# One encoder layer on one core: the mixer's projections as split fp32r pieces, with its other work cut into steps

## The chip, the cores and the metric

The kernel runs on one core of a Trainium2 chip. The core's engines work side by side, each through a queue of its own in order: TensorE (PE, with its weight loads as PEld), VectorE (DVE), ScalarE (ACT), GpSimd (POOL), and SyncE (SP), which here issues DMAs. The metric is the device time of one execution in microseconds (us): 2279.44 us before the change (median of 3 runs, 2277.18 to 2281.16).

## What is computed

One layer of a hybrid encoder on 256 tokens of width 2048, in float32:

```
h = rmsnorm(x);  p = h @ w_in                      # 5248 columns
z, q, k, v = split(p)
y_rwkv = rwkv7_bidir(z, ...)                       # 16 heads x 64, forward + backward delta-rule scans
y_attn = axial_gqa(q, k, v, ...)                   # 16 query heads, 4 kv heads, dim 64, softmax over 256
x = x + concat(y_rwkv, y_attn) @ w_out
x = x + peer_ffn(rmsnorm(x))                       # 8 heads, top 16 of 128 x 128 experts each
out = rmsnorm(x)

# in rwkv7_bidir, for each token and head (state is 64 x 64):
sa = state @ -kk;  state = state * w + outer(sa, ka) + outer(v, k);  y = state @ r
```

Everything up to `@ w_out` is called the mixer here, what follows PEER. In `peer_ffn` the kernel multiplies with all expert rows and weighs them by a gate, so PEER is two large dense products (`u` and `v`).

## The kernel before

**Layout.** Activations lie with features on the 128 partitions and the 256 tokens along the free axis. A weight block of 128 output columns is contracted over 2048 inputs in 16 steps k.

**The mixer before.** Its products are plain float32. `proj` (line 274) makes one block of 128 columns: four loads of 256 KB (`rw`), and 16 matmuls of a 128x128 weight with the 128x256 tokens `xy` into a PSUM tile `pj`. The trace has two records for each float32 matmul, so a block is 32 records. There are 40 such blocks of `w_in`; `proj_v` (335) does the work of two more for the value columns; `wout_block` (711) and `late` (787) do the 16 blocks of `w_out`, each contraction in four quarters, added one by one on DVE to the residual tiles `h`. The last quarter is `late`.

Between the projections stands the mixer's other work, small matmuls in float32 and DVE and ACT instructions:
- `shifted` (403): scale by 1/rms (`z`), then the centred token shift (`zk`, `zr`, `zv`), on DVE and ACT.
- `prep` (456), for each of 4 units of 4 heads, 2 directions and 2 halves (16 passes): decays (`sg`, `cs`, `Pt`, `iP`), in-context rates (`av`), scaled keys `AK` and queries `pk`, their chunk products, masks (`pk<-pr`, `Ld`, `L`) and transposes; results go to DRAM (`D`, `V`).
- `inverse` (545): a 32x32 triangular inverse, 30 dependent pairs of DVE instructions on tiles `h`; `merge` (562) makes 64x64 inverses from it with 128 small matmuls. Both run twice.
- `chain` (589): the scan over 4 chunks of 64 tokens, for two units (8 heads in both directions) at a time; each chunk loads `PK` and `VV` from DRAM and needs the state `N` of the chunk ahead. It runs twice (C0, C1). `epilogue` (645) is group norm, bonus and gate.
- `attend` (395): per group of 4 heads, `scores` and `values`: scores in PSUM, maximum on DVE, exponentials `pe` on ACT, transposes on PE, copy `pt` on ACT, product with the values.

**What sets the order in the mixer.** The string `ORDER` (line 39) gives the order in which these parts are written, and that order is the priority of a list scheduler in the compiler, which places each engine's instructions by its own estimate of their ends. Nothing in the mixer is ordered by hand.

**PEER.** From line 736 on the queues follow the order as written. The weights come in pieces of 512 KB (`raw`). A piece is split before use into two fp32r parts: ACT writes the rounded part `wH` (`wH<-raw`), POOL or DVE the rest `wL` (`wL<-raw,wH`). `mm3` (209) then makes a product from three fp32r matmuls, weight and token operand each in a high and a low part (high times high, high times low, low times high). `wide` (821) does it with a 512-column and a 256-column matmul. `go` (764) keeps `AHEAD` = 3 pieces split and `RAWB` = 4 more loaded ahead of the one in use.

Of the kernel before, what the change touches and what calls it, by code (L numbers as in the profile page):

```python
# [132 lines left out]

def body(tc, a, out, dbg={}):
    nc = tc.nc
    V, S, G, T = nc.vector, nc.scalar, nc.gpsimd, nc.tensor
# [97 lines left out]

# [7 lines left out]
    pss = bank("pt")[:, 0:2]  # L242
    pro = tc.tile_pool(name="pro", bufs=1, side="right")
    wp = pro.__enter__()
    xrs = [wp.tile([128, 4, 256], F, name="xr", bufs=4) for c in range(4)]
    for c in range(4):
        nc.sync.dma_start(xrs[c], a["xT"][:, 4 * c:4 * c + 4, :])
    nc.sync.dma_start(cst, a["cst"])
    for c in range(4):
        xr = xrs[c]  # L250
        tt(V if c < 2 else G, xA[:, 4 * c:4 * c + 4], xr,
           Pm("n1", 4 * c, 4)[:, :, None].to_broadcast([128, 4, 256]), OP.mult)
    for c in range(4):
# [3 lines left out]
        V.tensor_reduce(sm, sq.rearrange("p k t -> p t k"), axis=AX.X, op=OP.add)
        for b in range(2):
            mm(pss[:, b:b + 1], sm[:, b * 128:(b + 1) * 128], ones[:, 0:1], c + b == 0, c == 3)
    rstd = const.tile([128, 2, 1], F)  # L260
    rsqrt(wp, rstd[:, :, 0], pss, 2, 1.0 / 2048, 1e-6)
    psb = bank("pt")[:, :256]
    spread(psb, rstd.to_broadcast([128, 2, 128]))
    act(rstdb, psb)
    pro.__exit__(None, None, None)

    dr = pool("dr", 1, DRAM)
    ldp = pool("ldp", 1, side="right")
    rwc = pool("rwc", 1, side="right")
    at = pool("at", side="right")  # L270
    wk = pool("wk", 1)
    two = lambda p: p.rearrange("p (a b) -> p a b", a=2)

    def proj(n):
        p = pp.tile([128, 256], F, name="pj")
        for c in range(4):
# [5 lines left out]
    def headscale(pl, sq, scale, add, guard=None, tag="s2", bt="pr"):  # L282

        p = bank(bt)[:, :8].rearrange("p (b i h) -> p b i h", b=2, i=2)
        for b in range(2):
            for i in range(2):
                mm(p[:, b, i], sq[:, i, b * 128:(b + 1) * 128], bones[:, 0:128:64], b + i == 0, True)
        s1 = pl.tile([128, 8], F, name="s1")
        rsqrt(pl, s1, p.rearrange("p b i h -> p (b i h)"), 8, scale, add, guard)
        s2 = pl.tile([128, 8, 64], F, name=tag, bufs=2 if tag == "w2" else 1)  # L290
        V.tensor_copy(s2, s1[:, :, None].to_broadcast([128, 8, 64]))
        s2 = s2.rearrange("p (b i h) n -> p b i (h n)", b=2, i=2)
        p = bank(bt).rearrange("p (a b) -> p a b", a=2)
        for i in range(2):
            spread(p[:, i], s2[:, :, i])
        return p


    rope = at.tile([128, 768], F, name="rope")
    RP = {"rot": rope[:, 0:128], "swp": rope[:, 128:256], "cos": rope[:, 256:512], "sin": rope[:, 512:768]}  # L300
    c2 = lambda n: RP[n][:, None, :].to_broadcast([128, 2, 256])

    zA = at.tile([128, 5, 2, 256], F, name="zA")
    kW = at.tile([128, 2, 256], F, name="kW")
    vA = at.tile([128, 2, 256], F, name="vA")

    def proj_attn(n):
        for i in range(2):
            p = proj(30 + 2 * n + i)
            tt(V, zA[:, n, i], p, rstdb, OP.mult)  # L310

    def qk_block(n, w, bt):

        zs = zA[:, n]
        q = at.tile([128, 2, 256], F, name="aq")
        act(q, zs, AF.Square)
        V.tensor_scalar(zs, zs, w, None, op0=OP.mult)
        tt(V, zs, zs, headscale(at, q, 1.0 / 64, 1e-6, bt=bt, tag="aq"), OP.mult)
        p = bank(bt)
        mm(p, RP["rot"], zs)  # L320
        q = at.tile([128, 2, 256], F, name="aq")
        tt(V, q, two(p), c2("sin"), OP.mult)
        tt(V, zs, zs, c2("cos"), OP.mult)
        tt(V, zs, zs, q, OP.add)

    def keys(bt):
        nc.sync.dma_start(rope, a["rope"])
        qk_block(4, Pm("kn"), bt)
        p = bank(bt)
        mm(p, RP["swp"], zA[:, 4])  # L330
        act(kW, two(p))
        tap("kA", zA[:, 4])
        tap("vA", vA)

    def proj_v():
        pv2 = [pp.tile([128, 256], F, name="pj") for _ in range(2)]
        for c in range(8):
            W = wload(a["wv"][:, 2 * c:2 * c + 2, :].rearrange("p a (b n) -> p (a b) n", b=2))
            W = W.rearrange("p (a b) n -> p a (b n)", b=2)
            for b in range(2):  # L340
                for k in range(2):
# [6 lines left out]
    pes, sms, pys = {}, {}, {}

    def scores(e, bt):  # L350
        g, hq = divmod(e, 4)
        i, h = divmod(hq, 2)
        s = slice(64 * h, 64 * h + 64)
        kt = zA[s, 4, g // 2] if g % 2 == h else kW[s, g // 2]
        if hq == 0:
            sms[g] = at.tile([128, 2, 4], F, name="sm", bufs=2)
        p = two(bank(bt))
        for b in range(2):
            mm(p[:, b], zA[s, g, i, b * 128:(b + 1) * 128], kt)
        mx = at.tile([128, 2], F, name="mx", bufs=2)  # L360
        V.tensor_reduce(mx, p, axis=AX.X, op=OP.max)
        V.tensor_scalar(mx, mx, -0.125, None, op0=OP.mult)
        pes[e] = at.tile([128, 2, 256], F, name="pe", bufs=2)
        for b in range(2):
            act(pes[e][:, b], p[:, b], AF.Exp, scale=0.125, bias=mx[:, b:b + 1],
                accum_out=sms[g][:, b, hq:hq + 1])
# [53 lines left out]

# [828 lines left out]
```

## Time and profile before

| | us |
|---|---|
| median of the runs | 2279.44 |
| the profiled execution | 2277.42 |
| its span, first to last instruction | 2275.6 |
| PE busy in the span | 2214.7 |
| DVE busy | 1223.4 |
| ACT busy | 961.8 |
| POOL busy | 823.6 |
| first product of PEER (a matmul on `hh`) | at 664.5 |

The profile's page groups the instructions by line, engine and operation; most lines are those of helpers (158 for matmuls, 161 for ACT, 164 for DVE and POOL), so the tile names tell the groups apart. Busy times of PE are those of pipelined instructions that overlap, and say less than the distance from one start to the next.

### The profile page before, as it was taken

To read this page: it belongs to the slowest core of one execution; us is meant where nothing else is said; L and a number is where in the kernel's file an instruction comes from. 1 tells how busy PE (TensorE), PEld (TensorE's weight loads), DVE (VectorE), ACT (ScalarE), POOL (GpSimd) and SP (SyncE) were. 2 spreads that over 40 slices of the span, in tenths; PEclk is the share of its full clock that TensorE was granted. 3 is DMA by queue.
4 is the path that set the end of the run, shared out by engine and by line. 5 is a ranking of instruction groups with operands and counts; after the bars stand their busy time and mean duration, and the time that the engine had idled before them with its cause. 6 is when DMAs were issued, how large, how long until landed. Compare 5 with 4: busy or idle time off the path is not lost.

```text
span 2275.6 us, 33493 instructions
## 1 busy us (share of the span) xinstructions
PE 2214.7 (97%) x12790; PEld 1883.2 (83%) x12790; DVE 1223.4 (54%) x2556; ACT 961.8 (42%) x1479; POOL 823.6 (36%) x377
## 2 busy tenths in 40 slices
PE   7999799899999999999999999999999999999997
PEld 6888688787878889999888888888888888887886
DVE  3365875675367788887443352342533433456654
ACT  1121222323137755555544444444444444444443
POOL 0000000000027600000755555555555555556554
PEclk9999799699999999999999999999999999999999
DMA  5465364275455546666756666566566566676674
GB/s 196 148 188 174 127 196 146 82 240 174 138 183 170 174 160 221 213 209 215 240 189 205 203 194 209 190 203 212 187 211 205 185 211 205 194 229 212 207 209 133
DMA packets 188832, 431.50 MB, mean 190 GB/s; under 512 B 39680, under 2 KB 82304, under 8 KB 184448
## 3 DMA queue, kind: packets, MB, share of 16 engines
q1 hardware_dynamic: 177376, 409.96, 57.2%
q10 hardware_dynamic: 11296, 19.40, 2.5%
q8 instruction: 101, 1.65, 0.3%
q14 instruction: 59, 0.48, 0.1%
HBM read 391.55 MB, written 37.75 MB: 189 GB/s over the span
## 4 chain that ended last, share of the span: by engine, by line
PE 91%; DVE 5%; ACT 1%; DMA 1%; issue 1%; ACTq 0%; SPq 0%; DVEq 0%
PE pc L158 37%; PE pj L158 33%; PE pr L158 19%; PE pt L158 1%; DVE wL L164 1%; DVE oh L164 1%; ACT wH L161 0%; PE pr L532 0%; DMA VV<-V 0%; DVE pk L164 0%; DVE xy L164 0%; DVE hh L807 0%; DVE AK L164 0%; DVE h L164 0%; DVE rs L164 0%
## 5 line engine op out<-in xcount | busy, mean ns | idle before, releaser
L164 POOL TENSOR_TENSOR wL<-raw,wH 128x1024 fp32r<-128x1024 f32 x328 | 798.3, 2438 | 1018.5 <-ACT wH L161 1011.9
L161 ACT ACTIVATE wH<-raw 128x1024 fp32r<-128x1024 f32 x544 | 575.4, 1060 | 456.3 <-PE pc L158 282.8
L164 DVE TENSOR_TENSOR wL<-raw,wH 128x1024 fp32r<-128x1024 f32 x216 | 274.1, 1269 | 347.4 <-ACT wH L161 347.3
L158 PE MATMUL pr<-hh,wH 128*128 128x512 f32 x1152 | 409.3, 396 | 0.2 <-ACT wH L161 0.2
L158 PE MATMUL pj<-hh,wH 128*128 128x512 f32 x1152 | 408.0, 395 | 1.5 <-DVE hh L807 1.3
L158 PE MATMUL pc<-wH,aH 128*128 128x512 f32 x1024 | 406.7, 397 | 1.1 <-DVE acc L164 1.1
L158 PE MATMUL pc<-wH,aL 128*128 128x512 f32 x1024 | 404.8, 395 | 0.0
L158 PE MATMUL pc<-wL,aH 128*128 128x512 f32 x1024 | 402.0, 393 | 0.0
L158 PE MATMUL pj<-xy,rw 128*128 128x256 f32 x1664 | 382.6, 386 | 0.0
L158 PEld LDWEIGHTS pj<-xy,rw 128*128 128x128 f32 x1664 | 316.6, 193 | 49.6 <-issue 4.7
L158 PE MATMUL pr<-hh,wL 128*128 128x256 f32 x1152 | 323.1, 281 | 1.4 <-DVE wL L164 1.4
L158 PE MATMUL pj<-hh,wL 128*128 128x256 f32 x1152 | 322.1, 280 | 0.0
L158 PEld LDWEIGHTS pj<-hh,wH 128*128 128x128 f32 x1152 | 216.4, 188 | 48.4 <-DVE hh L807 2.0
L158 PEld LDWEIGHTS pr<-hh,wH 128*128 128x128 f32 x1152 | 217.2, 189 | 46.6 <-ACT wH L161 0.5
L158 PEld LDWEIGHTS pc<-wH,aL 128*128 128x128 f32 x1024 | 192.2, 188 | 48.3
L158 PEld LDWEIGHTS pc<-wL,aH 128*128 128x128 f32 x1024 | 192.3, 188 | 46.6
L158 PEld LDWEIGHTS pc<-wH,aH 128*128 128x128 f32 x1024 | 192.2, 188 | 46.1 <-DVE acc L164 1.5
L158 PEld LDWEIGHTS pr<-hh,wL 128*128 128x128 f32 x1152 | 217.2, 189 | 2.4 <-DVE wL L164 2.4
L158 PEld LDWEIGHTS pj<-hh,wL 128*128 128x128 f32 x1152 | 216.5, 188 | 0.4
L164 DVE TENSOR_TENSOR acc<-pc,acc 128x512 f32<-128x512 f32 x128 | 86.2, 688 | 131.6 <-PE pc L158 131.6
L504 POOL COPY vp<-zv 128x256 f32<-128x256 f32 x16 | 7.7, 482 | 307.2 <-PE pr L509 177.2
L161 ACT ACTIVATE gc<-pc 128x512 f32<-128x512 f32 x64 | 69.1, 1080 | 72.8 <-PE pc L158 72.8
(294 smaller groups left out, 1995.2 us busy)
## 6 DMA issues: line engine op xcount, KB each, us to landing
raw<-u SPq DMA_DIRECT2D x256, 512.0 KB, 4.1
raw<-v SPq DMA_DIRECT2D x256, 512.0 KB, 3.9
rw<-win SPq DMA_DIRECT2D x160, 256.0 KB, 2.8
PK<-D ACTq DMA_DIRECT2D x16, 1024.0 KB, 7.9
raw<-wpq SPq DMA_DIRECT2D x32, 512.0 KB, 4.3
gd<-gc SPq DMA_DIRECT2D x16, 1024.0 KB, 4.9
h<-gd SPq DMA_DIRECT2D x32, 512.0 KB, 6.9
D<-pk SPq DMA_DIRECT2D x16, 896.0 KB, 4.4
```

The lines of the kernel that those rows point to most:

```text
L158: T.matmul(o, l, r, start=start, stop=stop, skip_group_check=True)
L161: S.activation(o, i, f, **kw)
L164: e.tensor_tensor(o, x, y, op=op)
L504: G.tensor_copy(vp[:, 1:5], c4(rev(zv[:, i], d)))
```

## The change

The mixer's large products become pieces of the same kind as PEER's, in the same list `todo`, ahead of PEER's. The tokens are kept as high and low fp32r parts (`xS`), and so are the mixer's outputs (`yS`). A piece of `w_in` is half of a block (8 of the 16 steps k): `x_block` runs 24 matmuls of 256 columns. There are 80 pieces for the 40 blocks, 4 for the value columns, 16 for the attention half of `w_out` (`out_attn`), and 8 each for the scan quarters (`out_scan`, `late`): 116 pieces. DVE writes `wL` for all of them, ACT `wH`.

All other work of the mixer is written as generators. `step` runs one piece (`go(True)`) and then one turn of every task in the list, so that the written order, and with it the scheduler's priority, mixes one piece with one turn of each task. `go(True)` leaves the `wL` of the pieces rounded meanwhile to `rest_pieces`, which comes after the tasks' turns.

Beside that: the scalings of `sg`, `av` and a new `a2` go from DVE to POOL; the `Ld` blocks (`Ld<-pc`) and the copies of `merge` go from DVE to ACT; the `AK` and `pk` products are made for all 128 partitions at once instead of by halves, and of `pk` the second half goes to DRAM in more DMAs; the decay weights (`lo`) and the chunks `PK`, `VV` are loaded a unit or a chunk ahead, by SP instead of ACT's queue; `inverse` takes turns of 3 or 4 of its pairs; attention runs as one pipeline over 16 heads (scores, transposes a turn later, values a turn after that). While the query columns 32 to 37 are projected, a piece is used in every second step. `out_attn` waits for the attention outputs, `out_scan` for C0, `late` for C1. The residual adds of the last quarter (`residual`) come a step after the piece whose sums they take. PEER is as before.

The core of the diff (new code, then the lines that it replaces):

```diff
+    def round_piece():
+        i = at_["split"]
+        H = stp.tile([128, 8, 128], R, name="wH", bufs=AHEAD + 1)
+        L = stp.tile([128, 8, 128], R, name="wL", bufs=AHEAD + 1)
+        act(H, raws[i])
+        hl[i] = (H, L)
+        at_["split"] += 1
+    def rest_pieces():
+        while at_["rest"] < at_["split"]:
+            i = at_["rest"]
+            H, L = hl[i]
+            tt(todo[i][2], L, raws.pop(i), H.bitcast(F), OP.subtract)
+            at_["rest"] += 1
+    def step(late=False):
+        now = list(ends)
+        ends.clear()
+        V.n = 0
+        for t in now:
+            next(t)
+        if late:
+            go(True)
+        for t in list(tasks):
+            tasks.remove(t)
+            if next(t, StopIteration) is not StopIteration:
+                tasks.append(t)
+            if V.n >= STEP:
+                break
+        tasks[:0] = now
+    def x_block(n, c, evict):
+        def use(H, L):
+            if c == 0:
+                xp[n] = bank()[:, :256] if n == 24 else pj()
+            for k in range(8):
+                mm3(xp[n], H[:, k], L[:, k], xS[:, c + k, 0], xS[:, c + k, 1], c + k == 0, c + k == 15)
+            if c:
+                ends.append(evict(n, xp.pop(n)))
+        return from_rows(a["win"][n, :, c:c + 8, :]), use, V
+    def residual(o):
+        for n, p in o:
+            tt(V, x2(n), p, x2(n), OP.add)
+            act(hh[:, n, 0], x2(n), AF.Copy, scale=Pm("n2", n))
...
+        yield
+        for n, _ in o:
+            rest(n)
...
+        G.tensor_scalar(sg, sg, 0.5, 0.5, op0=OP.mult, op1=OP.add)
+        G.tensor_scalar(av, av, 0.5, 0.5, op0=OP.mult, op1=OP.add)
+        G.tensor_scalar(a2, av, Pm("ka", j), ka1[:, j:j + 1], op0=OP.mult, op1=OP.add)
...
+    while at_["use"] < NO or ("C", 1) not in done:
+        i = at_["use"]
+        ok = i < NO
...
+        if NX <= i < NA:
+            ok = "A" in done and bool(x2T)
+        elif NA <= i < NO:
+            ok = ("C", 0) in done
...
+        if "at2" in pools and i < NX and slots % 2:
+            ok = False
+        step(ok)
+        rest_pieces()
-ORDER = ("U0 P0 U1 P1 U2 I0 P2 U3 Q4 M0 P3 V K Q0 Q3 A0 Q1 Q2 A1 W C0 I1 A2 M1 C1 A3 w2 w3 w0")
-    def proj(n):
-        p = pp.tile([128, 256], F, name="pj")
-        for c in range(4):
-            W = wload(a["win"][n, :, 4 * c:4 * c + 4, :])
-            for k in range(4):
-                mm(p, W[:, k], xA[:, 4 * c + k], c + k == 0, c + k == 6)
-        return p
```

**How the queues move.** First DVE, in the middle of the third unit's preparation. Before, DVE has there only the preparation, the evictions of the projections (`z`, `zv`) and the second half of a norm:

```order
L164 TENSOR_TENSOR kk<-kk,pr 128x512
L479 TENSOR_SCALAR sg<-sg 128x256
L480 TENSOR_SCALAR av<-av 128x256
L482 SCALAR_TENSOR_TENSOR cs<-cst,sg 128x256
L164 TENSOR_TENSOR sg<-kk,av 128x256
L164 TENSOR_TENSOR z<-pj,rstdb 128x256
L492 TENSOR_SCALAR av<-av,prm,der 128x256
L164 TENSOR_TENSOR pk<-kk,Pt_361 64x4x64 x2
L164 TENSOR_TENSOR pk<-zr,Pt_361 128x4x64
L164 TENSOR_TENSOR AK<-sg,iP 64x4x64 x2
```

Now, in the same preparation, the rows are these (`h` is the inverse of the first two units, `wL` the split of a piece that TensorE uses up to four pieces later):

```order
L149 TENSOR_TENSOR wL<-raw,wH 128x1024
L149 TENSOR_TENSOR h_2458<-h_2456 128x30
L149 SCALAR_TENSOR_TENSOR cs_2464<-cst,sg_2395 128x256
L149 SCALAR_TENSOR_TENSOR zv<-z,prm,zv 128x255
L149 TENSOR_TENSOR h_2456<-h_2456,h_2458 128x30
L149 TENSOR_TENSOR av_2396<-kk,av_2396 128x256
L149 TENSOR_TENSOR ks<-zk,a_2397 128x256
```

The two scalings and the `av` line with `prm,der` have left DVE; a `wL` stands between the preparation's instructions about once in eight, and the steps of the inverse are strewn among them.

Second TensorE, in the scan of the last two units (C1). Before, eight or so matmuls of a `w_out` block (`pj<-xy,rw`) stand between one step of the scan and the next:

```order
L158 MATMUL pc<-X,PK 64x64 x16
L158 MATMUL pj<-xy,rw 128x256 x8
L158 MATMUL pc<-VV,PK 64x64
L158 MATMUL pc<-PK,VV 64x64
L158 MATMUL pc<-VV,PK 64x64 x15
L158 MATMUL pc<-PK,VV 64x64 x15
L158 MATMUL pj<-xy,rw 128x256 x8
```

Now, from the end of C0's epilogue to the first steps of C1, the rows between two pieces are small matmuls only: attention's (`pe`, `vA`, `kW`, `zA`), the epilogue's gate (`sgl`) and the scan's (`VV`, `X`):

```order
L177 MATMUL pc<-sgl,g_5514 128x256 x4
L177 MATMUL pc<-VV,PK 64x64 x7
L177 MATMUL pt<-vA,pt 128x64 x4
L177 MATMUL pc<-VV,PK 64x64 x4
L1004 MATMUL pr<-cst,pe 128x128
L177 MATMUL pc<-VV,PK 64x64 x4
L1004 MATMUL pr<-cst,pe 128x128 x3
L177 MATMUL pr<-zA_3460,zA_5033 128x256 x2
L177 MATMUL pc<-VV,PK 64x64
L1047 MATMUL pr<-cst,zA_3680 128x128 x4
L177 MATMUL pt<-vA,pt 128x64 x4
L177 MATMUL pc<-X,PK 64x64 x16
```

The `w_out` matmuls that lay between the scan's steps now come after them: 84 pieces of 116 stand ahead of this place, 2 among the rest of attention and the steps of C1 up to its last chunk, and 30 behind.

More of the change, by code (lines that the diff above doesn't have):

```diff
@@ L348, in body @@
[L348 to L366, printed above, removed]
@@ L771, in go @@
         while at_["split"] < min(len(todo), i + AHEAD + 1):
-            split_piece()
+            round_piece()
+        if not late:
+            rest_pieces()
         todo[i][1](*hl.pop(i))
@@ new lines, in body @@
+    tokens(0)
+    split_piece()
+    tokens(1)
+    tokens(2)
+    split_piece()
+    tokens(3)
+    rstd = const.tile([128, 2, 1], F)
+    dr = pool("dr", 1, DRAM)
+    wk = pool("wk", 1)
+    go()
+    go()
+    sms = [squares(0), squares(1)]
+    go()
+    sms += [squares(2), squares(3)]
+    go()
+    pss = bank("pt")[:, 0:2]
+    for c in range(4):
+        for b in range(2):
+            mm(pss[:, b:b + 1], sms[c][:, b * 128:(b + 1) * 128], ones[:, 0:1], c + b == 0, c == 3)
+    rsqrt(const, rstd[:, :, 0], pss, 2, 1.0 / 2048, 1e-6)
@@ new lines, in body, with load_lo, operand_tasks @@
+    half, turn = set(), set()
+    fin = {}
+    def load_lo(u, d):
+        los[u, d] = wk.tile([96, 2, 256], F, name=f"lo{d}")
+        nc.sync.dma_start(los[u, d], a["l2"][u][:, d::2])
+    def operand_tasks():
+        last = {}
+        for d in range(2):
+            load_lo(0, d)
+        for u in range(4):
+            while not (("head", u) in done and "tl" in done):
+                yield
+            for d in range(2):
+                for i in range(2):
+                    while i in last and last[i] not in half:
+                        yield
+                    last[i] = (u, i, d)
+                    tasks.append(operands(u, i, d))
+                    for _ in range(3):
+                        yield
+                if u < 3:
+                    load_lo(u + 1, d)
@@ new lines, in inverses @@
+    def inverses():
+        for k in range(2):
+            while fin.get(2 * k + 1, 0) < 4:
+                yield
+            rate = IRATE[k]
+            for n, _ in enumerate(inverse(k)):
+                if n % rate == rate - 1:
+                    yield
+            yield
+            yield from merge(k)
+    rope = at.tile([128, 768], F, name="rope")
+    nc.sync.dma_start(rope, a["rope"])
+    RP = {"rot": rope[:, 0:128], "swp": rope[:, 128:256], "cos": rope[:, 256:512], "sin": rope[:, 512:768]}
@@ new lines, in chains, with first_chunks, reorder @@
+    def chains():
+        for k in range(2):
+            yield from chain(k)
+    first = {}
+    def first_chunks():
+        for k in range(2):
+            while not (("M", k) in done and "ck" in pools and (k == 0 or ("last", 0) in done)):
+                yield
+            first[k] = chunk_load((2 * k, 2 * k + 1), 0)
+    x2T = []
+    x2 = lambda n: x2T[n // 4][:, n % 4]
+    yS = []
+    def reorder():
+        while ("P", 3) not in done:
+            yield
+        close(wk)
+        pools["at2"] = pool("at2", side="right")
+        pools["rwc"] = pool("rwc", 1)
+        pools["ck"] = pool("ck")
+        while ("M", 1) not in done:
+            yield
+        for k in range(4):
+            x2T.append(hole(k, [128, 4, 256]))
+            nc.sync.dma_start(x2T[k], a["xT"][:, 4 * k:4 * k + 4])
@@ L963, in body @@
         if n == 0:
-            rest(15)
+            step()
             square_sum(11)
```

1090 lines of the change are left out of this document (633 added, 457 removed).

## The prediction

> **What bounds the kernel now.** First the page's busy shares, then the windows cut at the stages, then the rows of the groups, the waits and the timeline.
>
> ```profile
> span 2275.6 us, 33493 instructions
> PE 2214.7 (97%) x12790; PEld 1883.2 (83%) x12790; DVE 1223.4 (54%) x2556; ACT 961.8 (42%) x1479; POOL 823.6 (36%) x377
> ```
>
> Windows (columns: length; busy us of PE, PEld, DVE, ACT, POOL; granted clock; DMA share; GB/s):
>
> ```profile
> 0.00:14.40 14.40, 2.00 (x9) 1.95 (x10) 9.36 (x13) 5.50 (x5) 4.94 (x6) 1.00 0.88 310
> 262.00:400.00 138.00, 137.43 (x959) 117.33 (x958) 96.65 (x283) 34.50 (x86) 6.05 (x12) 1.00 0.57 172
> 400.00:460.00 60.00, 52.06 (x223) 42.96 (x222) 39.92 (x120) 17.95 (x52) 2.49 (x4) 0.66 0.30 94
> 460.00:632.00 172.00, 167.56 (x1994) 140.25 (x1993) 95.30 (x255) 39.62 (x87) 0.00 (x0) 0.99 0.57 175
> 664.40:2275.60 1611.20, 1590.93 (x8308) 1351.33 (x8308) 846.74 (x1549) 806.68 (x1108) 794.60 (x330) 1.00 0.63 200
> 0.00:664.40 664.40, 623.77 (x4482) 531.88 (x4482) 376.66 (x1007) 155.16 (x371) 28.95 (x48) 0.95 0.52 164
> ```
>
> The mixer takes 664.4 us, and TensorE is busy in 623.8 of them: it is the bound there, with DVE at 57% and ACT at 23%. PEER's 1611.2 us are not touched by the change. So the question is what TensorE's 664 us become. The windows of the tiles `rw` and `raw` alone, the float32 products of the mixer, give PE and PEld:
>
> ```profile
> 0.00:664.40 664.40, 397.50 (x1728) 328.40 (x1728) 0.95 0.52 164
> ```
>
> ```profile
> 0.00:664.40 664.40, 28.36 (x128) 24.09 (x128) 0.00 (x0) 2.10 (x2) 3.71 (x2) 0.95 0.52 164
> ```
>
> Together 425.9 us, 58 blocks of 32 records. The rest of PE's busy time, 623.8 - 425.9 = 198 us, is small matmuls, which the change keeps in number and columns. About 8 of it I put down to the low clock (an estimate: half of the window 400 to 460 is small work, at 0.66), so 190 at full clock.
>
> **TensorE's part.** The rate of the new products stands in PEER, where fp32r matmuls of 256 columns occur between those of 512:
>
> ```profile
> 1257.89 0.39 PE L158 MATMUL pj<-hh,wH 128*128 128x512 f32 x1
> 1258.12 0.28 PE L158 MATMUL pj<-hh,wL 128*128 128x256 f32 x1
> 1258.12 0.19 PEld L158 LDWEIGHTS pj<-hh,wH 128*128 128x128 f32 x1
> 1258.23 0.40 PE L158 MATMUL pj<-hh,wH 128*128 128x512 f32 x1
> ```
>
> And one row of the chain, 16 such pairs:
>
> ```profile
> 1079.69 5.55 PE pj L158 x32
> ```
>
> Start to start, 512 columns take 0.23 us and 256 take 0.11 (1258.12 to 1258.23); a pair is 5.55 / 16 = 0.347, which leaves 0.114. The next weights load meanwhile. In the mixer this becomes a stream of 256 alone, a load every 0.11 us, which no row shows at this size. The nearest is four transposes, with four loads and four matmuls of 128 columns in 0.44 us (109.92 to 110.36; PEld first):
>
> ```profile
> 109.71 0.57 PEld L232 LDWEIGHTS pr<-cst,ks 128*128 128x128 f32 x4
> ```
>
> ```profile
> 109.92 0.60 PE L232 MATMUL pr<-cst,ks 128*128 128x128 f32 x4
> 110.36 1.03 PE L158 MATMUL pr<-tl,lo 96*128 96x256 f32 x4
> ```
>
> That is a load each 0.11 us, so 0.1135 should hold: 24 x 0.1135 = 2.72 us a piece, 116 pieces 316 us, against 425.9 now. Bounds: 0.11 (both rows) to 0.19 (the load's whole record, if nothing hid it). The Trainium skill, "TensorE: Matmul & The Clock Gate", Part 3, says that weight loads overlap matmuls in flight only when the row groups differ; here they are all the full array, so each matmul would pay its load as well. The rows above disagree: the load of 1258.12 lies under the matmul of 1258.12. I keep that rule as a rival.
>
> The start gets later: ahead of the first block's second half DVE must make 16 low parts of the tokens, 3 sums and 2 splits.
>
> ```profile
> L807 DVE SCALAR_TENSOR_TENSOR hh<-h,prm,hh x16: 483/485/2332, 638.7 to 671.5; 128x256 fp32r<-128x256 f32 x16
> L257 DVE TENSOR_REDUCE xs<-xq 128x256 f32<-128x1024 f32 x4 | 7.5, 1900 | 0.0
> L164 DVE TENSOR_TENSOR wL<-raw,wH x216: 1210/1225/3421, 789.4 to 2248.1; 128x1024 fp32r<-128x1024 f32 x108
> L161 ACT ACTIVATE wH<-raw 128x1024 fp32r<-128x1024 f32 x544 | 575.4, 1060 | 456.3 <-PE pc L158 282.8
> ```
>
> 16 x 0.485 + 3 x 1.9 + 2 x 1.23 = 15.9 us, from about 5 us on (DVE was busy 9.4 of the first 14.4); it is done at 21, and the two pieces that PE could have ended at 14.4 + 5.4 end at about 23: +3. Work on PE: 14.4 + 3 + 316 + 190 = 523 us.
>
> **DVE's part.** It takes on 116 splits at 1.225 us (the median in its row): 142 us. Rows that leave it or shrink, in the mixer:
>
> ```profile
> L164 DVE TENSOR_TENSOR Ld<-pr,cst 32x128 f32<-32x128 f32 x64 | 18.3, 285 | 4.7 <-ACT L L161 3.8
> L164 DVE TENSOR_TENSOR AK<-sg,iP 64x256 f32<-64x256 f32 x32 | 13.8, 430 | 0.4
> L164 DVE TENSOR_TENSOR pk<-kk,Pt 64x256 f32<-64x256 f32 x32 | 13.4, 418 | 0.2
> L492 DVE TENSOR_SCALAR av<-av,prm,der 128x256 f32<-128x256 f32 x16 | 6.7, 422 | 0.5
> L479 DVE TENSOR_SCALAR sg<-sg 128x256 f32<-128x256 f32 x16 | 4.7, 292 | 34.9 <-ACT sg L161 34.9
> L577 DVE COPY h<-pt 32x512 f32<-32x512 f32 x8 | 5.5, 690 | 9.0 <-PE pt L158 8.9
> ```
>
> `Ld` to ACT (-18, two multiplies of a split's size instead, +2.5). 64 half-height `AK` and 32 `pk<-kk` instructions become 32 and 16 of full height at the same price (-14 and -7). The scalings of `sg` and `av`, alike, and the `av` line go to POOL (2 x 4.7 + 6.7: -16); merge's 16 copies at 0.69 to ACT (-11); 16 residual adds fewer at 0.42 (-7). The rest is about even. Sum -70: DVE gets 377 + 142 - 70 = 449 us, against 523 on PE. ACT gets 155 + 116 x 1.06 and, with what it takes over, some 50: 328. POOL's some 40 and ACT bind nothing. SP takes the chunk loads from ACT's queue and issues four `D` writes for each one before:
>
> ```profile
> PK<-D ACTq DMA_DIRECT2D x16, 1024.0 KB, 7.9
> D<-pk SPq DMA_DIRECT2D x16, 896.0 KB, 4.4
> ```
>
> ```profile
> 567.76 1.15 PE L158 MATMUL pc<-X,PK 64*64 64x64 f32 x32
> 582.29 1.15 PE L158 MATMUL pc<-X,PK 64*64 64x64 f32 x32
> ```
>
> I cost both at nothing: pieces are loaded up to seven ahead, some 19 us of PE's work, as cover, and a chunk is asked for one chunk ahead, which is 14.5 us in C1 now (the same step of two chunks, 567.76 and 582.29), more than the 7.9 us. Without that cover a write that waits for `pk` holds the `raw` loads behind it on SP, and each chunk costs up to 8 us.
>
> **Waits.** A split stands in DVE's queue among instructions that wait for PE, and PE waits for the split. I have counted both queues along their order with these prices (DVE's times 0.94, since the same count of the kernel before gives 387 us where the trace has 362). Up to piece 64 PE has 226 us of work and DVE 221; from 84 to 88 PE has 67, of it 56 small matmuls, and between the 88th and the 89th split DVE has 48 us without any. So three terms:
> - Pieces 16 to 64, both engines equally loaded, each in order: +10 (0 to +60; in the window 262 to 400 DVE was busy for 97 of 138 us, 0.70).
> - The place without pieces: the scan of C1, C0's epilogue and attention. In the window 400 to 460, attention with few projections between, the granted clock was 0.66, and in its middle 0.50 (row below). Some 50 of the 56 us lie there, and at 0.66 are 76: +26 (0 to +50, at clock 1 and at 0.50).
> - The last quarter, with the rows below: DVE makes 16 adds of 0.42, 16 rests of 0.485, 4 sums of 1.94 and 4 splits beside it, 27 us, against 22 on PE: +5. The adds a step later cost nothing: the next piece's matmuls cover them.
>
> ```profile
> 420.00:440.00 20.00, 19.43 (x74) 15.46 (x75) 12.10 (x31) 8.59 (x29) 0.89 (x1) 0.50 0.13 48
> ```
>
> ```profile
> L164 DVE TENSOR_TENSOR h<-pj,h 128x256 f32<-128x256 f32 x56 | 23.6, 422 | 42.6 <-PE pj L158 42.0
> L810 DVE TENSOR_REDUCE sm<-sq 128x256 f32<-128x1024 f32 x4 | 7.8, 1938 | 0.0
> ```
>
> The Trainium skill, same page, Part 1, has the clock at half after an idle window of about 3.4 us, with no value between; by that rule all 50 us might run at half, and the term would be +50. The rows with 0.50 and with the mean of 0.66 allow both.
>
> The sum: 523 + 10 + 26 + 5 = 564 us for the mixer, 100 less than 664.4. The span becomes 2175.6, the execution, 1.8 us longer (2277.4 for 2275.6), 2177.4. The median of the runs was 2.0 above the profiled execution, so **2179**. What is late next is PE itself, by its work.
>
> **Rivals.**
> - *The order fits and PE never waits.* For it: PE is at 97% now under the same scheduler, and C0 and C1 run there among other work at clock 0.99. Mixer 523 + 5, time 2143.
> - *DVE becomes the bound.* If it can't be busier than 0.70 through pieces 16 to 92 (338 us by the count), these take 483 us, the sparse place included, with 64 us of PE ahead and 76 behind: 623, so 2238. For it, the waits of DVE for PE and ACT (us in all, times, longest):
>
> ```profile
> DVE z L164 <- PE pj L158: 58.9, 18, 4.9
> DVE sg L479 <- ACT sg L161: 34.9, 13, 6.3
> ```
>
> Against it: they cost nothing there, since DVE had time.
> - *PE and DVE take turns (slower).* Where a split stands behind an eviction that waits for the piece in PE, the lead of four pieces is lost, and DVE's work up to piece 84 (313 us) is added to PE's, not hidden. The slack is 664 - 523 - 31 = 110 us, so it decides from 35% of the 313. At half the mixer takes 523 + 156 + 31 = 710, time 2325. Against it: `wL` stands up to four pieces ahead in the order.
> - *Weight loads are not hidden (slower).* 2784 x 0.188 instead of 316 is +207: 2386. This is the rule above as a mechanism of this kernel; a stream of 256 columns might run into it though pairs don't.
> - *The change doesn't do what it says*: the scheduler could have pulled the pieces apart from the tasks. The order shows them mixed, but for the one place; 2 in 100 for no change.
>
> **How the numbers follow.** Forecast 0.57 (2160 to 2210), PE never waits 0.17, DVE bound 0.16, turns 0.05, loads 0.03, no change 0.02. The range 2143 to 2240 reaches to the second and third case. A measurement of this kernel can tell about 0.2%, 4.6 us, from no change: faster 0.90, same 0.02, slower 0.08.
>
> **What would show it.** PEER's first product at about 564 us; `pj<-xy,wH` start to start 0.11 us, 24 in 2.7 us; PE busy over 90% up to piece 84; a window of some 75 us with clock under 0.8 and few pieces; DVE near 445 us busy ahead of PEER. Wrong would be: loads that stretch the piece over 3 us; PE waiting for `wL` in over 50 us; or a PEER stage whose length differs by over 5 us.

## The result, and the profile after

The changed kernel takes **2208.2 us** (median of 4 runs, 2205.8 to 2211.1) beside 2279.2 (4 runs), a ratio of **0.9689** (95% interval 0.9672 to 0.9706). That is faster, as forecast, but by 71 us and not by 100. One execution in the experiments, of the kernel with a stagger of 2, took 4233.4 us, nearly twice the others, and is in no number below. The profiled execution took 2207.99 us. Its page:

```profile
span 2206.2 us, 35765 instructions
PE 2150.8 (97%) x13782; PEld 1869.6 (85%) x13782; DVE 1280.7 (58%) x2491; ACT 1128.7 (51%) x1752; POOL 851.1 (39%) x417
```

PE has 64 us less, DVE 57 and ACT 167 us more. The windows, cut where pieces 2, 16, 64, 84 and 88 of the 116 (counted from 0) begin, at the end of the preparation (333.0), at the last quarter (562.4) and at PEER's first product (columns as above):

```profile
0.00:24.90 24.90, 11.41 (x60) 10.95 (x61) 17.68 (x31) 16.30 (x26) 0.20 (x4) 0.93 0.77 265
...
72.00:253.30 181.30, 176.75 (x1566) 171.23 (x1565) 161.32 (x357) 121.39 (x273) 43.85 (x62) 1.00 0.73 212
253.30:333.00 79.70, 71.10 (x716) 62.21 (x714) 59.02 (x134) 47.57 (x102) 10.82 (x20) 0.90 0.67 184
...
443.60:496.90 53.30, 53.25 (x731) 45.63 (x727) 27.27 (x59) 20.07 (x45) 0.00 (x0) 1.00 0.35 113
496.90:562.40 65.50, 65.50 (x527) 64.12 (x526) 45.86 (x85) 26.92 (x31) 0.00 (x0) 1.00 0.53 167
562.40:588.80 26.40, 24.32 (x202) 23.91 (x200) 20.66 (x33) 16.71 (x34) 3.19 (x2) 1.00 0.40 126
588.80:2206.20 1617.40, 1597.91 (x8310) 1358.61 (x8310) 846.75 (x1551) 805.58 (x1107) 793.04 (x330) 1.00 0.63 199
0.00:588.80 588.80, 552.90 (x5474) 510.98 (x5474) 433.99 (x941) 323.12 (x647) 58.07 (x88) 0.97 0.62 186
```

The mixer takes 588.8 us where it took 664.4: 75.6 less, with PE busy in 552.9 of them, DVE in 434, ACT in 323. PEER takes 1617.4, 6.2 more than before. The pace of the new products stands in the timeline:

```profile
26.33 0.40 PE L177 MATMUL pj<-xy,wH 128*128 128x256 f32 x2
26.57 0.28 PE L177 MATMUL pj<-xy,wL 128*128 128x256 f32 x1
26.69 0.40 PE L177 MATMUL pj<-xy,wH 128*128 128x256 f32 x2
```

Three matmuls take 0.36 us, 0.120 each, a piece 2.88 us. So 2784 of them are 334 us, against 426 for the float32 products: 92 us of TensorE's work are gone, and the mixer lost 76.

A second reading matters more. Three marks of the mixer's own chain: the last `yb` (the preparation's end; `xy<-pr,zv` in the kernel before), the first and last `X` (the scan's first and last chunk), and PEER's first product. The kernel before, then the changed one (columns: shortest, median and longest duration in ns, first and last start):

```profile
L161 ACT ACTIVATE X<-pc x8: 597/598/604, 472.6 to 594.3; 128x512 f32<-128x512 f32 x8
...
L164 DVE TENSOR_TENSOR xy<-pr,zv x4: 691/692/693, 184.0 to 454.5; 128x512 f32<-128x512 f32 x4
```

```profile
L180 ACT ACTIVATE X<-pc x8: 592/597/600, 350.4 to 486.1; 128x512 f32<-128x512 f32 x8
...
L149 DVE TENSOR_TENSOR yb<-pr,zv x4: 678/683/684, 141.6 to 333.2; 128x512 f32<-128x512 f32 x4
...
L177 PE MATMUL pj<-hh,wH x368: 387/396/774, 588.9 to 895.2; 128*128 128x512 f32 x184
```

The scan starts 122.2 us earlier (472.6 to 350.4). From its first to its last chunk, both runs of the scan take 135.7 us, 14.0 more, and from its last chunk to PEER it is 102.8 us where it was 70.2, 32.6 more, with 28 of the 32 output pieces beginning only after 496 us. -122.2 + 14.0 + 32.6 = -75.6. So the whole gain lies ahead of the scan, whose start follows the preparation's end by 17 to 18 us in both kernels, and more than a third of it is given back behind. This says where the time went and not yet what set it.

### The profile page after: what moved, and what is told of

Its sections match the earlier page's. It is cut to its first block, busy times and chain, and to the rows that moved or that the text cites. A ratio compares the mean times of both kernels' runs of the same rounds, so it can differ in the third digit from the quotient of the medians.

```text
span 2206.2 us, 35765 instructions
## 1 busy us (share of the span) xinstructions
PE 2150.8 (97%) x13782; PEld 1869.6 (85%) x13782; DVE 1280.7 (58%) x2491; ACT 1128.7 (51%) x1752; POOL 851.1 (39%) x417
## 4 chain that ended last, share of the span: by engine, by line
PE 88%; DVE 7%; ACT 2%; DMA 1%; issue 1%; POOL 0%; SPq 0%; DVEq 0%; ACTq 0%
PE pc L177 38%; PE pj L177 27%; PE pr L177 20%; DVE wL L149 2%; DMA D<-pk 1%; DVE h L149 1%; PE pt L177 1%; DVE oh L149 1%; DVE pk L149 1%; ACT wH L180 1%; PE pr L1004 0%; DVE rs L149 0%; DVE hh L149 0%; ACT h L180 0%; DVE zA L149 0%
## 5 line engine op out<-in xcount | busy, mean ns | idle before, releaser
L180 ACT ACTIVATE wH<-raw 128x1024 fp32r<-128x1024 f32 x660 | 696.3, 1058 | 538.6 <-PE pc L177 273.3
L149 DVE TENSOR_TENSOR wL<-raw,wH 128x1024 fp32r<-128x1024 f32 x332 | 412.6, 1244 | 389.7 <-ACT wH L180 386.0
L177 PE MATMUL pj<-hh,wH 128*128 128x512 f32 x1152 | 414.0, 398 | 0.0
L177 PE MATMUL pj<-xy,wH 128*128 128x256 f32 x1632 | 313.7, 292 | 15.6 <-ACT wH L180 10.5
L177 PEld LDWEIGHTS pj<-xy,wH 128*128 128x128 f32 x1632 | 261.8, 196 | 23.4 <-ACT wH L180 11.2
L177 PE MATMUL pj<-xy,wL 128*128 128x256 f32 x816 | 234.7, 288 | 1.9 <-DVE wL L149 1.9
L177 PEld LDWEIGHTS pj<-xy,wL 128*128 128x128 f32 x816 | 159.6, 196 | 2.7 <-DVE wL L149 2.3
```

The costliest lines, as they stand in the source:

```text
L149: return f(*args, **kw)
L177: T.matmul(o, l, r, start=start, stop=stop, skip_group_check=True)
L180: S.activation(o, i, f, **kw)
```

## The experiments

**Theory before the runs:** TensorE's work sets the mixer, but for a stretch with DVE at its limit. **Rival:** the chain of dependent small work, preparation, scan, attention, sets it. Each run is compared with the kernel before on its own chip; the changed kernel stands at 2208.2 and 0.9689.

### One product of three left out

```diff
+    def mm2(ps, sH, sL, mH, mL, start, stop):
+        mm(ps, sH, mH, start, False)
+        mm(ps, sL, mH, False, stop)
-                mm3(xp[n], H[:, k], L[:, k], xS[:, c + k, 0], xS[:, c + k, 1], c + k == 0, c + k == 15)
+                mm2(xp[n], H[:, k], L[:, k], xS[:, c + k, 0], xS[:, c + k, 1], c + k == 0, c + k == 15)
```

The same stands in the other pieces, here and in the next two. 

> The mixer's pieces leave out the product of the weights' high part with the tokens' low part (16 of 24 matmuls of 256 columns in each of the 116 pieces); loads, splits, evictions and the order stay. Theory: TensorE's own work sets the mixer, except in the stretch 180 to 260 us where DVE was busy in 19.5 of each 20 us. 928 matmuls fewer at 0.120 us are 111 us; the 48 pieces 16 to 64 can give little, since DVE had 161 us of work in those 181, so I expect 65 to 90 us less in the mixer, first PEER product at 500 to 525 us, time 2118 to 2143. Rival 'TensorE alone': the whole 111, product at 478, time 2097. Rival 'the chain of small work and DVE sets the mixer, the pieces only fill in': under 40 us less, time above 2168.

Measured: 2180.3 us (0.9568, 0.9549 to 0.9587). 111 us of work gone, 28 gained: the chain's rival. The windows cut at piece 72, piece 76 and PEER:

```profile
0.00:231.40 231.40, 203.63 (x1599) 191.47 (x1600) 206.16 (x419) 165.97 (x333) 49.12 (x66) 0.96 0.77 241
231.40:330.40 99.00, 52.96 (x495) 40.21 (x494) 65.78 (x178) 40.86 (x97) 9.92 (x20) 0.64 0.45 125
330.40:558.00 227.60, 215.19 (x2454) 189.80 (x2455) 156.39 (x346) 116.22 (x216) 2.79 (x2) 0.92 0.57 181
```

The same cuts in the changed kernel:

```profile
0.00:301.30 301.30, 279.09 (x2537) 268.76 (x2538) 243.48 (x520) 190.30 (x393) 50.84 (x79) 0.98 0.68 202
301.30:335.10 33.80, 26.82 (x166) 21.18 (x164) 29.01 (x72) 16.35 (x37) 4.04 (x7) 0.79 0.77 219
335.10:588.80 253.70, 246.98 (x2775) 221.04 (x2774) 161.51 (x350) 116.47 (x218) 3.19 (x2) 0.97 0.52 163
```

Up to piece 72 the time fell by 69.9 us, just the 72 x 0.96 of work: TensorE bounds that stretch. Then pieces 72 to 76 took 99 us, not 34. They need tiles in memory that the preparation holds, and it ends at 329.0 here, at 333.2 there. Of the 70 us, 65 were waited away. From piece 76 on, 40 pieces gave 26 of their 38 us.

### Half the columns in one product of three

```diff
+    def mmh(ps, sH, sL, mH, mL, start, stop):
+        mm(ps, sH, mH, start, False)
+        mm(ps[:, 0:128], sH, mL[:, 0:128], False, False)
+        mm(ps, sL, mH, False, stop)
-                mm3(xp[n], H[:, k], L[:, k], xS[:, c + k, 0], xS[:, c + k, 1], c + k == 0, c + k == 15)
+                mmh(xp[n], H[:, k], L[:, k], xS[:, c + k, 0], xS[:, c + k, 1], c + k == 0, c + k == 15)
```

> The same product is made for 128 of the 256 columns only (the rest is left out); the number of matmuls and of weight loads stays at 24 in a piece. Theory 'columns set the pace': 256 columns at 0.120 us are 0.47 ns a column, so 8 of the 24 matmuls cost half, a piece takes 2.88 - 8 x 0.06 = 2.4 us, and 65 to 90 hundredths of 116 x 0.48 = 56 us are gained: 25 to 50 us less than the changed kernel's 2208. Rival 'a weight load each 0.11 to 0.12 us sets the pace' (as in the four transposes of 128 columns, 0.44 us): a piece stays at 2.8 to 2.9 us and the time within 8 us of 2208.

Measured: 2209.2 us (0.9695, 0.9672 to 0.9717), the rival. The timeline of this kernel:

```profile
120.18 0.34 PE L177 MATMUL pj<-xy,wH 128*128 128x256 f32 x2
120.30 0.19 PEld L177 LDWEIGHTS pj<-xy,wL 128*128 128x128 f32 x1
120.36 0.34 PE L177 MATMUL pj<-xy,wL 128*128 128x256 f32 x1
120.41 0.31 PEld L177 LDWEIGHTS pj<-xy,wH 128*128 128x128 f32 x2
...
120.54 0.34 PE L177 MATMUL pj<-xy,wH 128*128 128x256 f32 x2
120.66 0.19 PEld L177 LDWEIGHTS pj<-xy,wL 128*128 128x128 f32 x1
```

From one `wH` row to the next (its two matmuls are the full and the short one) it is 0.36 us still, with a sixth fewer columns: `wL` starts at 120.36, soon after the short one, and the next product only 0.18 us behind it. From one load of `wL` to the next (120.30 to 120.66) there are three weight loads, one each 0.12 us: they set the pace.

### The steps alone, with plain float32 products

The steps stay here together with the moves between engines and the loads ahead; only the split products go.

```diff
+    def mmp(ps, s, m, start, stop):
+        mm(ps, s.bitcast(F), m.bitcast(F), start, stop)
-                mm3(xp[n], H[:, k], L[:, k], xS[:, c + k, 0], xS[:, c + k, 1], c + k == 0, c + k == 15)
+                mmp(xp[n], H[:, k], xS[:, c + k, 0], c + k == 0, c + k == 15)
```

> The changed kernel with all its steps, its loads ahead and its late quarter, but with plain float32 products in the mixer: ACT copies each piece as before, DVE makes no low parts of weights, tokens or mixer outputs. Theory: the gain is that of the fp32r products, and the rearrangement by itself gives nothing: PE's products go from 116 x 2.88 = 334 us back to the 426 of the kernel before, DVE's 143 us of splits go, so the mixer takes 588.8 + 92 - (0 to 25 of waits for DVE) = 656 to 681, time 2275 to 2300, that is within 1% of the kernel before. Rival 'the rearrangement brings a good part of it' (chunk loads ahead, fewer DVE instructions, attention spread among pieces): mixer under 640, time under 2259.

Measured: 2239.4 us (0.9827, 0.9811 to 0.9844). The rival: the steps without fp32r give 39 of the 71 us. The scan's row, and the mixer's window:

```profile
L180 ACT ACTIVATE X<-pc x8: 592/597/599, 357.9 to 513.2; 128x512 f32<-128x512 f32 x8
```

```profile
0.00:629.10 629.10, 609.47 (x4547) 519.33 (x4547) 301.57 (x804) 325.24 (x649) 45.68 (x89) 0.98 0.57 175
```

The scan starts at 357.9, only 7.5 us later than with fp32r: the steps alone bring it forward by 115 us. Here TensorE is busy in 609 of 629 us: with float32 the steps leave it few gaps. fp32r then takes off 92 us of work and 40 of mixer time, of which PEER gives 7 back (1610.3 here; why, below).

### fp32r alone, in the old order

```diff
-            W = wload(a["win"][n, :, 4 * c:4 * c + 4, :])
+            H, L = split(a["win"][n, :, 4 * c:4 * c + 4, :])
             for k in range(4):
-                mm(p, W[:, k], xA[:, 4 * c + k], c + k == 0, c + k == 6)
+                mm3(p, H[:, k], L[:, k], xH[:, 4 * c + k], xL[:, 4 * c + k], c + k == 0, c + k == 6)
```

`split` is ACT's rounding and DVE's rest on tiles of 128x512. 

> The kernel before, with its own order and loads, but with fp32r high and low parts for the projections of the tokens (42 of its 58 blocks; the output projection stays float32). On TensorE 308 us of float32 products become 84 x 2.88 = 242, so 66 us less; DVE takes on some 113 us. Theory 'the two parts of the change add up': the steps alone gave 39 of 70 us, so fp32r alone should give the rest, 31, and for 42 of 58 blocks some 15 to 30: time 2250 to 2265. Rival 'fp32r alone gives nearly all of its work back, the steps are needed for little': 50 us or more, time under 2230. Rival 'in the old order DVE's splits stand behind its waits for PE, and the gain is lost': within 10 us of the kernel before, or slower.

Measured: 2255.7 us (0.9902, 0.9886 to 0.9919): 23 us, within what two parts that add up should give for 42 of the 58 blocks. 66 us of work gone give a third back, as in the steps (31 of 92).

### DVE's splits

```diff
-        return from_rows(a["win"][n, :, c:c + 8, :]), use, V
+        return from_rows(a["win"][n, :, c:c + 8, :]), use, G if c and n < 24 else V
```

> Low parts of every second piece of the 24 unit blocks (24 of 116) are made on POOL (2.4 us each, as in PEER) in place of DVE (1.23): 30 us of DVE's work go, nearly all between 60 and 330 us. Theory 'DVE is the bound in 180 to 260 (19.5 of 20 us busy) and holds up the preparation of the last unit': mixer 10 to 25 us shorter, time 2183 to 2198. Rival 'TensorE's work is the bound anyway': within 5 us of 2208. Rival 'POOL's slower splits, behind its own scalings and waits for ACT, hold the pieces up': PE waits for wL more than its 2 us now, and the time is 2213 to 2230.

Measured: 2219.9 us (0.9736, 0.9719 to 0.9753), slower than the changed kernel: the third case. The group of POOL's splits from 60 to 330 us:

```profile
L183 POOL TENSOR_TENSOR wL<-raw,wH 128x1024 fp32r<-128x1024 f32 x20 | 50.9, 2543 | 54.4 <-ACT wH L180 54.4
```

The splits take twice DVE's time and wait for ACT (54.4 us in all), and POOL's scalings of `sg` and its copies `vp`, links of the preparation, stand behind them: it ended at 343.8, not 333.2. TensorE did not wait for `wL` more than before; that part of the expectation was wrong.

The trace shows a second possible cause. While POOL splits, DVE's instructions that read two tiles in SBUF, the on-chip memory of the tiles, stand still:

```profile
167.30 2.55 POOL L183 TENSOR_TENSOR wL<-raw,wH 128x1024 fp32r<-128x1024 f32 x1 [1.52 <-ACT wH L180]
170.17 2.62 POOL L183 TENSOR_TENSOR wL<-raw,wH 128x1024 fp32r<-128x1024 f32 x1 [0.32 <-ACT wH L180]
...
167.50 2.63 DVE L149 TENSOR_TENSOR ks<-ks,a 128x256 f32<-128x256 f32 x1
170.45 2.62 DVE L149 SCALAR_TENSOR_TENSOR ks<-ks,der,zr 128x256 f32<-128x256 f32 x1
```

In the changed kernel these two take 0.42 and 0.48 us. Here each ends 0.28 us after the split, and behind most of the 24 splits one DVE instruction is stretched so. DVE's busy time in the mixer rose from 434.0 to 443.9 us, though splits of 24 x 1.23 = 29 us had left it. So DVE was not relieved, and this run doesn't tell what a less loaded DVE would bring, nor how much of the 12 us is due to which of the two causes.

### The loads and the last quarter

```diff
+                nxt = chunk_load(us, c + 1)
                 for h in range(2):
                     V.tensor_copy(nxt[1][own[h], :, :, h], N[own[h]])
```

The load at the step's head goes in return. 

> The changed kernel, but the decays and inputs of the scan's next chunk are asked for in the step that needs them, not one chunk ahead. Six such loads remain in the two scans. Theory 'from the last preparation at 330 us to 497 us the chain of attention and scan sets the time, not TensorE's pieces': each of the 6 loads adds its 4 to 8 us to the scan, of which those beside attention's own chain may be hidden: 10 to 35 us slower than the changed kernel, 2218 to 2243. Rival 'TensorE has other work beside it': within 6 us of 2208, as I costed it in the prediction with its cover.

```diff
-            ends.append(residual(o))
+            r = residual(o)
+            next(r)
+            ends.append(again(r))
```

The adds, the first half of `residual`, now run in the piece's own step; `again` runs the second half in the next. 

> The changed kernel, but the last output quarter is added in the step of its own piece, not a piece later. Theory of the prediction 'DVE bounds the last quarter, 27 us for 22 of PE, and the later adds keep it from waiting for PE': at once, each of the 8 steps has DVE wait for its piece's last product before the next split, 0.5 to 1.5 us, so the stage gets 4 to 12 us longer, time 2212 to 2220. Rival 'the cover is not needed': the stage stays at 26 to 28 us and the time within 4 us of 2208.

Measured: 2206.4 us (0.9688, 0.9671 to 0.9705) and 2209.4 us (0.9688, 0.9665 to 0.9711). Neither part can be told from nothing; the rivals hold in both. The last quarter at once:

```profile
570.70:598.50 27.80, 24.15 (x203) 24.04 (x202) 25.07 (x35) 16.13 (x32) 4.77 (x2) 1.00 0.44 146
```

27.8 us against 26.4: at most 1.4 for the later adds.

### What holds the preparation

```diff
-                    for _ in range(3):
+                    for _ in range(2):
```

> The changed kernel, but the preparation's 16 operand tasks start every second step, not every third. With a third of TensorE's projection work gone the preparation still ended at 330 us, so its own chain sets that time. Theory 'the number of steps paces it': it ends 10 to 30 us earlier, attention and scan with it, and the mixer gets 8 to 25 us shorter, time 2183 to 2200. Rival 'DVE, 19.5 of 20 us busy in 180 to 260, or each task's wait for the buffers of the one before, paces it': within 5 us of 2208, and a wait for the buffers stands where the steps stood.

Measured: 2216.5 us (median of 3; 0.9728, 0.9709 to 0.9748), slower, which neither case had: more tasks at once don't end it earlier (339.0). What does? The waits of the changed kernel from 215 to 272 us, then its chain of waits there:

```profile
POOL vp L769 <- PE pr L780: 32.8, 1, 32.8
```

```profile
256.51 2.01 DVE h L149
258.56 1.98 PE pr L177 x64
260.54 0.59 PE pr L656 x4
```

For 32.8 us the preparation's next copy `vp` waits for transposes on PE. These stand behind `merge` (258.56), which waits for the inverse on DVE (`h`, to 258.5).

```diff
-IRATE = (3, 4)
+IRATE = (1, 4)
```

> The changed kernel, but one of the inverse's rounds per step for the first half of the units, not three. In the changed kernel the operands of the preparation stop between 222 and 267 us: their transposes stand in TensorE's queue behind the merge of the first inverse, whose 31 rounds of two dependent instructions DVE ends at 258 us; in the kernel with two of three products they stop from 217 to 270, at the same place. Theory 'this chain, and neither TensorE's nor DVE's sum of work, sets the end of the preparation': with the merge behind the last unit's operands (in the order it moves from piece 65 to 76) the preparation ends 20 to 40 us earlier, TensorE doesn't run out of pieces at 304, and the mixer gets 10 to 30 us shorter, time 2178 to 2198. Rival 'DVE's sum of work': the preparation still ends after 325 and the time is within 5 us of 2208. Rival 'the first scan, which waits for the merge, takes its place': the scan starts later and the time is 2208 to 2225.

Measured: 2209.3 us (0.9703, 0.9684 to 0.9722), the second rival. The mechanism held and the gain did not come. The preparation ended 20 us earlier, the scan did not start earlier:

```profile
L149 DVE TENSOR_TENSOR yb<-pr,zv x4: 673/678/684, 140.1 to 313.5; 128x512 f32<-128x512 f32 x4
...
L180 ACT ACTIVATE X<-pc x8: 589/597/599, 352.9 to 494.1; 128x512 f32<-128x512 f32 x8
```

```profile
360.00:380.00 20.00, 15.61 (x274) 12.99 (x273) 19.08 (x49) 5.09 (x13) 0.00 (x0) 0.85 0.70 228
380.00:400.00 20.00, 18.49 (x272) 15.04 (x272) 7.25 (x12) 10.54 (x20) 0.00 (x0) 0.50 0.34 92
400.00:420.00 20.00, 20.00 (x251) 17.35 (x246) 5.43 (x22) 5.89 (x13) 0.00 (x0) 0.54 0.53 146
```

The merge now comes at 314 to 338, and the load of the first chunk waits until its results are stored; then the second inverse fills DVE (busy for 19.08 of 20 us), PE runs dry and stands at half clock. Two more edits on top of this one:

```diff
-        yield from close_chain(k, us, y)
+        tasks.append(close_chain(k, us, y))
```

> As the run with one round a step, and the epilogue of the first scan is a task of its own, so that the second scan doesn't wait for it. In the changed kernel TensorE is busy for 15.9 of 20 us in 420 to 440, at clock 0.74, between the two scans. Theory 'chain': that place closes and 5 to 15 us more are gained, time 2165 to 2190. Rival 'the second scan's small products lie beside pieces in any case': within 4 us of the run with one round a step.

```diff
-IRATE = (3, 4)
+IRATE = (1, 2)
```

> As the run with one of the first inverse's rounds a step, and two rounds a step of the second inverse, not four. With one round a step the preparation ended at 314, not 333, and piece 80 was reached at 341, not 364 us; all of it was lost again in 360 to 420, where DVE was busy 19.1 of 20 us with the second inverse, TensorE ran dry and then stood at clock 0.50 to 0.54 for 40 us. Theory 'the bunch of the second inverse takes back what was gained': spread over twice the steps, TensorE has no idle stretch there and keeps its clock; 8 to 20 us less than the 2209 of that run, 2189 to 2201. Rival 'the second scan waits for that inverse': it starts later than 450 and the time is 2206 to 2222. Rival 'TensorE's sum of work from the preparation to the end': within 4 us of 2209.

Measured: 2209.5 us (0.9703, 0.9684 to 0.9723) and 2213.7 us (0.9719, 0.9701 to 0.9737). With the epilogue as a task of its own the two scans took 133.1 us, not 141.2, and the tail to PEER 102.7, not 96.5, which takes back most (the rival). The other edit did not spread the second inverse: DVE does its rounds from 345 to 382 us, where the run before had 344 to 380. What moved is the merge behind it, in TensorE's queue from 408 to 445 us instead of 382 to 412, and the second scan's first chunk comes at 463, not 450 us. That is the rival's outcome; the theory, an inverse in twice the steps, was not put to the test.

### Is the low clock a cause?

```diff
         if NQ < i < NX and "at2" not in pools:
             ok = False
+            p = pj()
+            for k in range(40):
+                mm(p, xS[:, k % 16, 0, 0:128], xS[:, k % 16, 0], k == 0, k == 39)
```

> The changed kernel with work added that computes nothing used: in each of the three steps in which pieces wait for the end of the preparation, 40 fp32r matmuls of 256 columns (4.8 us) into a bank that is read by no one. In 320 to 340 us TensorE was busy 13.9 of 20 us at clock 0.57. Theory 'the low clock costs time of its own': with the idle stretch filled the clock stays at 1, the small products there take half, and although 14 us of work are added the time is 0 to 8 us less, 2200 to 2208. Rival 'the low clock is only a sign that TensorE waits for the chain': the clock stays at 1, and the filler stands in front of the chain's own products, time 2208 to 2222.

Measured: 2219.0 us (0.9738, 0.9718 to 0.9758), the rival. The same window of the changed kernel, then with the filler:

```profile
320.00:340.00 20.00, 13.90 (x62) 9.73 (x60) 16.38 (x51) 6.34 (x18) 0.00 (x0) 0.57 0.78 219
```

```profile
320.00:340.00 20.00, 18.36 (x151) 16.36 (x149) 15.21 (x43) 7.16 (x16) 0.00 (x0) 1.00 0.38 109
```

The clock is 1.00, and of the 14.4 us of filler 11 show in the time: in this place the low clock is a sign of the wait, not its cause. The clock by itself can cost no more there than the 3 us that are missing.

### What the runs say together

From the rows above and their like in each run (us):

| | piece 72 begins | preparation ends | first to last chunk of the scans | from there to PEER | PEER begins |
|---|---|---|---|---|---|
| changed kernel | 301 | 333 | 350 to 486 (136) | 103 | 588.9 |
| two products of three | 231 | 329 | 342 to 479 (137) | 79 | 558.0 |
| plain float32 | 338 | 343 | 358 to 513 (155) | 116 | 629.1 |
| POOL splits | 324 | 344 | 362 to 507 (145) | 101 | 608.2 |
| half the columns in one of three | 297 | 335 | 346 to 492 (146) | 102 | 594.0 |
| stagger of 2 | 311 | 339 | 354 to 498 (144) | 101 | 598.4 |
| inverse 1 a step | 300 | 314 | 353 to 494 (141) | 97 | 590.6 |
| the same, epilogue its own task | 301 | 314 | 354 to 487 (133) | 103 | 589.5 |
| inverse 1 and 2 | 300 | 313 | 354 to 498 (144) | 96 | 593.6 |
| filler | 303 | 340 | 358 to 500 (142) | 101 | 601.3 |

The two scans take 133 to 146 us in every kernel with steps and fp32r, also where a third of TensorE's products are gone. So the theory as I stated it fell. The mixer is a chain: preparation and the first merge, scans of 136, then the output pieces, 103, where TensorE is the bound (busy for all of 496.9 to 562.4 us; with two products of three this part takes 24 us less). The scan starts 12 to 19 us after the preparation's end, except in the three runs with the slower inverse, where the merge comes last. In the first 301 us TensorE is the bound too, but that stretch ends ahead of the preparation.

What is not settled: what sets the 136 us of the scans. Attention's 16 heads stand in the same queues (its last scores at 477 us) and could be it; no run here took attention or scan out alone.

## Why the prediction was right, and why by 29 us too low

- **TensorE's work.** Products 316, measured 334: the pace was 0.120, not 0.1135. Half of that was in the row shown: 0.347 less 0.23 leaves 0.117, not 0.114. The 190 of small work and the 26 that the low clock adds agree with 552.9 - 334 - 3 (half speed at the start, below) = 216, in part by luck, since the low clock came in other places too. The start is 2 us off: piece 2 begins at 24.9, forecast 23.
- **Weight loads hidden.** Right; the rival with 2386 is out. The Trainium skill, "TensorE: Matmul & The Clock Gate", Part 3, lists that loads overlap matmuls only of other row groups; each matmul would then pay its load too, 0.19 + 0.11 = 0.30 us by the rows. The trace has 0.120, so the measurement decides against that line.
- **DVE.** 449 forecast, 434 measured. The rival that has it as the bound at 0.70 is out: from piece 16 to 64 it was busy for 161.3 of 181.3 us, 0.89. Turns between DVE and PE: PE waited for `wL` for 1.9 us in the mixer; that rival is out too.

```profile
PE pj L177 <- DVE wL L149: 1.9, 2, 1.4
```

- **Loads ahead at nothing, later adds at nothing, last quarter 27 us.** Right: 2206.4 and 2209.4 us without them, and 26.4 us.
- **Pieces up to 64.** 14.4 + 3 + 226 + 10 = 253, measured 253.3. The agreement is part luck: the pace alone is 64 x 24 x 0.0065 = 10, the whole of what I had set aside for waits.
- **The place without pieces, and a second one: the step that failed.** I had put it behind the first 84 pieces, with 67 us of work and 26 of low clock: 93. There it is: no piece runs from 408.5 to 443.6, and from the end of the 84th to the start of the 89th it is 88.4 us. The 88th split on DVE starts at 410.2, the 89th at 489.7. But the work in it was more and the low clock less: PE busy for 84.3 us, at a mean of 0.94. What I had at nothing is the other one: from 315.3 to 335.1, between the 76th piece and the 77th, TensorE waits for the preparation's end.

```profile
315.30:335.10 19.80, 12.82 (x57) 7.77 (x55) 17.69 (x51) 7.16 (x19) 0.00 (x0) 0.64 0.66 176
...
408.50:443.60 35.10, 31.03 (x233) 23.28 (x231) 21.29 (x69) 17.94 (x42) 0.00 (x0) 0.85 0.40 121
408.50:496.90 88.40, 84.28 (x960) 68.91 (x958) 48.56 (x128) 38.01 (x87) 0.00 (x0) 0.94 0.37 116
```

I had "counted both queues along their order", and a count per engine doesn't see a chain that goes from DVE's inverse to PE's merge, from there to transposes, POOL, ACT and back. From piece 64 to PEER I had 564 - 253 = 311 us; it took 335.5. Of these 24.5, 8 are the pace (52 pieces x 24 x 0.0065), and some 12 the wait ahead of the 77th piece (19.8 less 12.8 x 0.64 of small work, an estimate); the place behind the 84th gave 5 back. The other 9 I can't assign.
- **"What is late next is PE itself."** Wrong between 315 and 497 us: there it is the chain, and so the pace counts in part only. The run with two products of three shows that less work on PE up to piece 72 is waited away. PE was busy for 409.8 of the first 443.6 us, the "over 90%" that I had named as a sign, and the sign told nothing of this.
- **PEER untouched.** Over the 5 us that I had allowed: +6.2. Its matmuls run at 0.233 and 0.120 us start to start, where the kernel before has 0.230 and 0.117 (PE busy 1597.9 for 1590.9). The kernel before with fp32r in its mixer has 0.230 and 0.117 again, and the new one with plain float32 has 0.233 and 0.120, so the pace goes with the new kernel's code and layout, not with fp32r. Why is open. That the plain one's PEER is 7 us shorter even so lies in its first 31 us: PE is busy for all of them at clock 1.00, where the changed kernel waits 3.2 us for DVE's `sm` and has a clock of 0.89.
- **The total.** 24.8 more in the mixer and 6.2 in PEER: 2208.2 for 2179 (the median lies 0.2 us above the profiled execution, not 2.0). The pace makes 18 us (2784 x 0.0065), of which the 10 set aside for waits up to piece 64 covered more than half. The sum came near though the bound was misjudged in the middle, because TensorE is busy in 552.9 of the 588.8 us.
- **Where the gain comes from** I had not asked: the steps alone give 39 us, fp32r within them 31, fp32r alone in the old order 23.

## What to carry to other kernels

A sum of work per engine tells when an engine can't be the bound; it doesn't tell when the end comes if a chain crosses the engines, so mark the chain's ends in the trace (last preparation, first and last chunk) and subtract those first. Busy shares over 90% don't exclude such a chain. An experiment that takes a third of the busiest engine's work away shows in one run which stretches it bounds. To shorten one strand of several that end close together moves the wait to the next, as the run with two products and those with the slower inverse showed. And work moved to POOL can hold up DVE: look whether DVE's instructions beside it have grown.

## What the runs showed of the hardware

Weight loads of 128x128 start 0.12 us apart in this stream. They are hidden under matmuls of 256 columns; with one matmul of three cut to 128, three still take 0.36 us, so fewer columns than 256 a load brought nothing here.

A split on POOL (2.5 us in the mean) holds up a DVE instruction with two tiles in SBUF until 0.28 us after the split's end: 2.6 us for 0.4. Evictions from PSUM beside it keep their time (`z<-pj`, 0.41 us).

TensorE's pace was at half twice at the start: 0.213 us a matmul from 13 to 17 us, while the clock column has 1.00 there.

```profile
13.00:17.00 4.00, 4.00 (x20) 4.00 (x20) 4.00 (x8) 4.00 (x9) 0.00 (x0) 1.00 1.08 342
```

```profile
15.43 0.41 PE L177 MATMUL pj<-xy,wL 128*128 128x256 f32 x1
15.64 0.63 PE L177 MATMUL pj<-xy,wH 128*128 128x256 f32 x2
16.07 0.41 PE L177 MATMUL pj<-xy,wL 128*128 128x256 f32 x1
...
17.41 0.40 PE L177 MATMUL pj<-xy,wH 128*128 128x256 f32 x2
17.64 0.95 PE L177 MATMUL pt<-cst,xs 128*128 128x1 f32 x8
...
20.78 0.58 PE L177 MATMUL pj<-xy,wL 128*128 128x256 f32 x1 [0.53 <-DVE wL L149]
```

It was full at 17.4, and after three microseconds with only one-column matmuls and gaps half again from 20.8 to 24. Some 33 matmuls at 0.213 for 0.120 cost 3 us. The Trainium skill, "TensorE: Matmul & The Clock Gate", Part 1, gives some 3.4 us of activity to reach the full clock and one idle window of that length to lose it. Both stretches are near it (from 13 to 17 us, and 17.6 to 20.8), though the second is not idle throughout.
